# A two-layer hybrid transformer kernel: the residual stream held feature by token instead of token by feature

## The chip, the cores and the metric

The kernel runs on one core of a Trainium2 chip. The metric is device time in microseconds of one execution; lower is better. The kernel before took 808.06 us (median of 3 runs, 807.47 to 808.31). The core has five engines that run their own instruction queues in order: TensorE (PE in the rows; its weight loads are PEld), VectorE (DVE), ScalarE (ACT), GpSimd (POOL) and SyncE (SP), which issues the DMA transfers.

## The reference, cut to what matters

The input is 512 latent tokens `x` and 256 context tokens `ctx`, each of 1024 features, and one conditioning vector for each kind.

```
for layer in range(2):
    shift, scale, gate       = split(silu(c)     @ ada_w[layer] + ada_b[layer], 3)   # 1024 values each
    shift_c, scale_c, gate_c = split(silu(c_ctx) @ ada_w[layer] + ada_b[layer], 3)
    h_l = rmsnorm(x,  norm_g[layer]) * (1 + scale)   + shift
    h_c = rmsnorm(cx, norm_g[layer]) * (1 + scale_c) + shift_c
    # layer 0: latent attention (8 heads) and a bidirectional RG-LRU side by side
    # layer 1: 2-D neighbourhood attention (16 heads), latents only as output
    y_c, y_l = mixer(h_c, h_l)            # (mix * silu(gate path)) @ w_out, 1024 x 1024
    x  = x  + gate   * y_l
    cx = cx + gate_c * y_c                # layer 0 only
return rmsnorm(x, final_norm_g)           # rmsnorm: x * rsqrt(mean(x*x over features) + 1e-6) * g
```

## The kernel before, in words

All 768 tokens (512 latents `LAT`, then 256 context tokens `CTX`) go through the two layers at once. Products that need accuracy are made from operands split into a high part (`...h`, rounded for the fast float32 mode of TensorE) and a rest (`...l`): three matmuls (h x h, h x l, l x h) for each product. `split_raw` (L113) makes the parts of a weight: ScalarE the high part, VectorE or GpSimd the rest, in tiles from small rings (3 raw, 4 high, 4 low) in `t4` (L81). A raw slot is free when the rest has been made, and only then can SyncE issue the next weight's transfer into it.

**Startup.** The residual stream `x` lies token by feature: `x0` to `x5`, 128 tokens x 1024 features each. `norm0` (L327) squares and sums each tile on ScalarE along the features, takes the inverse root for all tokens on VectorE, and scales the tiles. `h_block` (L297) then makes, for each of 8 feature groups `j` and each kind of token, the tiles `hh` and `hl` (128 features x 768 tokens) that the projections read: four or two TensorE transposes into PSUM (`pst`, L302), ScalarE for the high part with scale `am` and shift `as`, VectorE for the difference (L310), GpSimd for the rest (L312). `am` and `as` come from `ada_cols` (L211): matmuls with a 32-column weight, four of them side by side on the columns of the array (`psada`, L205). The projections `z_t` (L134) keep a weight tile still and stream tokens: `psx0` to `psx3` (LRU input), `psg` (gates), `psn` (L578: attention's compressed q, k, v, with the token tile still and 416 weight columns streamed). One projection is 8 x 3 matmuls of 512 and of 256 columns.

**Gates.** `gate_rows` makes the layer's gate as rows (tokens' kind x 256 features), `gate_bc` (L253) spreads them over 128 partitions by a float32 matmul with a selecting weight (`psgt`), since the output projection leaves tokens on the partitions.

**Output projections and seam.** `out_mm` (L1109, `w0oy`, `w1oy`) keeps 128 tokens of the mixed activations `mh`/`ml` still and streams 256 weight columns; `out_add` multiplies by the gate and adds to `x` (two VectorE instructions). Between layer 0 and layer 1 (the "seam") `h_norm`, `x_scale` and `hb1` repeat norm and `h_block` for the new residual, by pairs of token tiles, while TensorE works on the projections left and on the first of layer 1 (`psv`, L1255, and `pskc`, `pskl`). After layer 1 the final norm ends each token tile and stores it, 4 transfers of 128 x 1024.

The order on each engine is that in which the scheduler puts the instructions of the program text; each engine runs its list in order. Tiles come from pools, so a new tile waits for the last reader of the one whose place it takes.

Of the kernel before, what the change touches and what calls it, by code (L numbers as in the profile page):

```python
# [37 lines left out]
NV = 111  # L38
# [5 lines left out]
def build(nc, tc, A, out, dbg=None):  # L44
# [76 lines left out]
    def split_w(name, src, shape, new=None, eng=V):  # L121
        return split_raw(name, load_w(name, src, shape, new), shape, new, eng)
# [25 lines left out]
    pt = pool("pt", 2, space=PSUM)  # L148
# [29 lines left out]
    junk0 = px.tile([128, D], BF16, name="junk0")  # L178
# [5 lines left out]

    sel = cst.tile([128, 2], F32, name="sel")
    iv = ident.rearrange("p (a b) -> p b a", b=32)
    V.tensor_reduce(sel, iv[:, 0:2], AX.X, ALU.add)
    selh = cst.tile([128, 2, 128], F32, name="selh")
    V.tensor_copy(selh, sel.unsqueeze(2).to_broadcast([128, 2, 128]))
    amul = [cst.tile([128, 8, 2], F32, name=f"am{l}") for l in range(2)]  # L190
    ashf = [cst.tile([128, 8, 2], F32, name=f"as{l}") for l in range(2)]
    badd = cst.tile([128, 48], F32, name="badd")
# [18 lines left out]
    def ada_cols(l, ch, raws, pp):  # L211
# [11 lines left out]
        j = 2 * ch  # L223

        def bc(t, i):
            return t[:, i : i + 2].unsqueeze(2).to_broadcast([128, 2, 2])

        V.tensor_tensor(ashf[l][:, j : j + 2], v[:, :, 0:2], bc(vec, V_ADAB + 24 * l + j), ALU.add)
        d = amul[l][:, j : j + 2]
        V.tensor_tensor(d, v[:, :, 2:4], bc(badd, 24 * l + 8 + j), ALU.add)  # L230
        V.tensor_tensor(d, d, bc(vec, V_NG + 8 * l + j), ALU.mult)

    def gate_rows(l, ch, pp, new=None, step=4):

        pm = ada_mm([ada_load(l, 8 + ch, new, step)], pp, f"psgr{l}_{ch}")
        S.activation(grows[:, ch], pm[:, :256], AF.Copy)
        gb = small("rows", f"gb{l}_{ch}", 256)[:2]
        SY.dma_start(gb, A["gateb"][l : l + 1, 256 * ch : 256 * ch + 256].to_broadcast([2, 256]))
        V.tensor_tensor(grows[0:2, ch], grows[0:2, ch], gb, ALU.add)

    def of3(tile):
        def new(n, s, dt, tag):
            if tag == "r" and tile is not th:
# [28 lines left out]
    def rsqrt1(y, a, b, scale):  # L272


        m, t = small("rm", "m1"), small("rt", "t1")
        V.tensor_scalar(m, a, b, scale * 2.0 ** 26, ALU.add, ALU.mult)
        V.tensor_scalar(t.bitcast(I32), m.bitcast(I32), 1, None, ALU.arith_shift_right)
        V.tensor_scalar(
            y.bitcast(I32), t.bitcast(I32), -1.0, float(0x5F3759DF - 2 ** 31), ALU.mult, ALU.add
        )  # L280
        for c in (3.0, 12.0, 768.0):
            V.scalar_tensor_tensor(t, y, m, y, ALU.mult, ALU.mult)
            V.scalar_tensor_tensor(y, t, c, y, ALU.subtract, ALU.mult)
# [1494 lines left out]
```

## Time and profile before

| | |
|---|---|
| median of 3 runs | 808.06 us |
| the profiled execution | 808.98 us |
| its span, first to last instruction | 807.0 us |
| mean granted TensorE clock | 0.986 |
| TensorE busy | 760.4 us, 94% of the span |
| VectorE / ScalarE / GpSimd busy | 505.6 / 419.2 / 167.6 us |

The page's chain that ended last is followed back from the last instruction through what released it; a share of it is a share of the span. Stages in the span: startup and first projections to about 70 us, LRU and the attention's inputs to 200, attention to 340, output projection of layer 0 to 425, the seam to 441, layer 1 to 740, its output projection to 797, the end to 807.

### The profile page before, as it was taken

The page shows a single profiled execution, that of the slowest core. Times are in us where ns is not written, and L with a number is a line of the kernel's source. Part 1 is how long each engine was busy: PE and PEld are TensorE (multiplying, and loading weights), DVE is VectorE, ACT ScalarE, POOL GpSimd, SP SyncE. Part 2 cuts the span into 40 slices and gives each one's busy share as a digit, 9 for nine tenths or more (in the row PEclk, how much of TensorE's full clock was granted, in tenths as well). Part 3 has the DMA queues.
Part 4 walks back from the last instruction along what each step waited for, and adds up shares of the span by engine and source line. Part 5 has one row for each costly group of instructions (what it writes and reads, how often), then busy time and mean ns, then how long its engine had stood idle before and what let it go on. Part 6 is the DMA issues. An engine that isn't in the chain of part 4 may idle for free.

```text
span 807.0 us, 13663 instructions
## 1 busy us (share of the span) xinstructions
PE 760.4 (94%) x5170; PEld 668.9 (83%) x5170; DVE 505.6 (63%) x1083; ACT 419.2 (52%) x820; POOL 167.6 (21%) x208
## 2 busy tenths in 40 slices
PE   3899999997999888999998999999999999999995
PEld 0568998886788678799997889988898889899995
DVE  4547499769478657624466446755654665568755
ACT  4344667763475668632275345544543554457523
POOL 2230000000142548540036002202110111021203
PEclk9999999998999999999999999999999999999998
DMA  8921124410453564145132244224522651335122
GB/s 335 372 88 70 53 91 131 156 41 0 108 141 105 150 183 146 60 135 179 54 141 95 81 129 131 71 73 114 149 92 79 196 170 31 104 115 144 54 79 105
DMA packets 32145, 95.86 MB, mean 119 GB/s; under 512 B 4288, under 2 KB 7504, under 8 KB 32080
## 3 DMA queue, kind: packets, MB, share of 16 engines
q1 hardware_dynamic: 32080, 94.99, 36.7%
q8 instruction: 41, 0.67, 0.3%
q14 instruction: 24, 0.20, 0.1%
HBM read 74.53 MB, written 4.19 MB: 98 GB/s over the span
## 4 chain that ended last, share of the span: by engine, by line
PE 80%; DVE 7%; DMA 5%; ACT 4%; issue 1%; POOL 1%; SPq 1%; DVEq 0%; ACTq 0%; POOLq 0%
PE psg L134 11%; PE w0oy L1109 8%; PE psv L1255 8%; PE psq L134 6%; PE pskl L134 6%; PE w1oy L1109 5%; PE psx L134 4%; PE psn L578 3%; PE pt L1372 3%; PE pskc L134 3%; PE s L745 3%; DMA ada_4r<-ada 2%; PE pg L134 2%; PE s L1331 2%; PE psada L205 2%; PE s L1332 2%
## 5 line engine op out<-in xcount | busy, mean ns | idle before, releaser
L701 POOL TENSOR_SCALAR p<-p,rc 128x512 f32<-128x512 f32 (+1 forms) x96 | 74.7, 780 | 325.9 <-DVE rc L700 313.1
L1339 ACT ACTIVATE p<-s,nm 128x512 f32<-128x512 f32 x64 | 43.9, 687 | 44.5 <-DVE nm L1337 33.3
L1375 DVE TENSOR_TENSOR ptl<-pt,pth 128x512 fp32r<-128x512 f32 x64 | 43.4, 685 | 20.4 <-ACT pth L1374 20.0
L1374 ACT ACTIVATE pth<-pt 128x512 fp32r<-128x512 f32 x64 | 37.2, 596 | 26.9 <-PE pt L1372 23.0
L1337 DVE CUSTOM_DVE_ANT_1 s<-s,bias 128x512 f32<-128x512 f32 x48 | 33.2, 697 | 20.4 <-PE s L1332 20.1
L747 DVE TENSOR_REDUCE nm<-s 128x1 f32<-128x768 f32 x32 | 30.4, 951 | 18.3 <-PE s L745 18.3
L1372 PE MATMUL pt<-ident,p 128*128 128x128 f32 x256 | 39.9, 272 | 0.0
L781 DVE TENSOR_TENSOR pt<-pt,pt 128x512 fp32r<-128x512 f32 x48 | 31.8, 682 | 8.3 <-ACT pt L780 7.8
L749 ACT ACTIVATE p<-s,nm 128x768 f32<-128x768 f32 x32 | 28.9, 903 | 14.1 <-DVE nm L747 14.0
L780 ACT ACTIVATE pt<-pt 128x512 fp32r<-128x512 f32 x48 | 27.2, 597 | 15.4 <-PE pt L818 15.1
L1331 PE MATMUL s<-k,q 128*128 128x256 f32 x128 | 34.0, 288 | 0.4 <-DMA q<-qx 0.4
L1372 PEld LDWEIGHTS pt<-ident,p 128*128 128x128 f32 x256 | 31.1, 140 | 3.6
L1332 PE MATMUL s<-k,q 128*128 128x256 f32 x128 | 33.5, 284 | 0.0
L1355 PE MATMUL po<-pth,v 128*128 128x256 f32 (+1 forms) x96 | 31.9, 338 | 0.0
L680 POOL TENSOR_TENSOR rb<-rb,ropet 128x512 f32<-128x512 f32 x2 | 2.6, 1278 | 138.3 <-DVE rb L678 138.3
L700 DVE RECIPROCAL rc<-rs 128x1 f32<-128x1 f32 x96 | 15.0, 158 | 25.3 <-ACT p L1339 15.5
L1356 PE MATMUL po<-ptl,v 128*128 128x256 f32 (+1 forms) x96 | 29.4, 323 | 0.0
L818 PE MATMUL pt<-ident,p 128*128 128x128 f32 x192 | 28.1, 273 | 0.5 <-DVE pt L781 0.4
L205 PE MATMUL psada<-ada_0r,c 128*32 128x256 f32 x128 | 13.3, 496 | 15.9 <-DMA ada_0r<-ada 9.9
L798 PE MATMUL po<-pt,v 128*128 128x256 f32 x96 | 26.7, 296 | 0.4 <-ACT pt L780 0.2
L799 PE MATMUL po<-pt,v 128*128 128x256 f32 x96 | 26.5, 300 | 0.6 <-DVE pt L781 0.5
L1331 PEld LDWEIGHTS s<-k,q 128*128 128x128 f32 x128 | 24.3, 190 | 2.1 <-DMA q<-qx 0.6
(911 smaller groups left out, 2735.5 us busy)
## 6 DMA issues: line engine op xcount, KB each, us to landing
ada_0r<-ada SPq DMA_DIRECT2D x24, 512.0 KB, 5.5
ada_4r<-ada SPq DMA_DIRECT2D x24, 512.0 KB, 10.1
q<-qx SPq DMA_DIRECT2D x32, 256.0 KB, 4.9
bias<-bias SPq DMA_DIRECT2D x16, 256.0 KB, 3.1
x<-xin SPq DMA_DIRECT2D x6, 512.0 KB, 10.5
xr<-xin SPq DMA_DIRECT2D x12, 256.0 KB, 5.2
x1d<-xr SPq DMA_DIRECT2D x4, 512.0 KB, 2.7
x<-x1d SPq DMA_DIRECT2D x4, 512.0 KB, 3.2
```

The costliest lines, as they stand in the source:

```text
L134: P.matmul(ps, a(k), b[k][:, c], start=(k == 0 and i == 0), stop=(k == nk - 1 and i == 2),)
L701: G.tensor_scalar(p, p, rc, 0.5, ALU.mult, ALU.mult)
L1109: P.matmul(ps[:, j], tok(a[k], t), b, start=(n == i == j == 0), stop=(n == 7 and i == 2), skip_group_check=True,)
L1255: P.matmul(ps, tok(a[k], t), b[:, k % 4], start=(k == 0 and i == 0), stop=(k == 7 and i == 2))
L1331: P.matmul(s[:, :256], lhs, kap, start=(i == 0), stop=False, skip_group_check=True)
L1332: P.matmul(s[:, 256:], lhs, k2[:, CTX], start=False, stop=(i == 1), skip_group_check=True)
L1337: V.tensor_tensor_reduce(sv, sv, bb, -1.0, 3e38, ALU.add, ALU.min, nm)
L1339: S.activation(p, s, AF.Exp, bias=nm, scale=-1.0, accum_out=rsum)
L1355: P.matmul(dst, vv, h, start=first, stop=False, skip_group_check=True)
L1372: P.transpose(ps[:, 128 * j : 128 * j + 128], p1[hd, b][:, 128 * c : 128 * c + 128], ident)
L1374: S.activation(h, ps, AF.Copy)
L1375: V.tensor_tensor(l, ps, f(h), ALU.subtract)
```

## The change

The residual stream is kept feature by token: `x0` to `x7` hold 128 features x 768 tokens, and the host lays out `xin` and takes the output that way (in the transposed shape 1024 x 512). What follows from it:

- **Norms.** ScalarE (two of eight tiles: GpSimd) squares the tiles, TensorE sums over features by matmuls with a 32-column tile of ones (`sq_sum`), `rs_bc` copies the sums, transposes them to tokens on the partitions (`r..t`), adds the four partial sums, takes the inverse root (startup and end: ScalarE's square root, reciprocal and one Newton step; seam: the three-step code of before), and transposes it back spread over 128 partitions (`r..b`) into `rsb`.
- **h_block.** No transposes: VectorE `x * a * rsb` in place, ScalarE adds the shift for `hh`, VectorE makes `hl`. GpSimd has no part in it.
- **Gates** are made as columns (`ada_gate`), like shift and scale; `gate_rows`, `gate_bc` and `psgt` are gone, and `out_add` is one VectorE instruction.
- **Output projections** keep 128 x 128 of the weight still and stream tokens: 512 at a time for layer 0's latents, 256 for its context and for layer 1, which goes in two halves of 256 tokens, each with its own norm and store (16 transfers of 128 x 256 in all).
- **Order.** All `x` loads come first. `psg8` is projected in the startup along with `psx0` and `psx1`. Layer 0's output goes latents first; the latent `hb1` stand among the context's projections, the context's among the first projections of layer 1. Some weight splits move (`w0o2`, `w0o3`, `w1o3`, the rest of `w1k0` to GpSimd).

```
+    def sq_sum(ps, sq, g, n):
+        for j, a in enumerate(sq):
+            P.matmul(ps[32 * j : 32 * j + 32, :n], ones, a, start=(g == 0), stop=(g == 1), skip_group_check=True)
+    def rsqrt1(y, v, scale, n, name):
+        m, t = small("rm", name + "m", n), small("rt", name + "t", n)
+        S.activation(t, v, AF.Sqrt, scale=scale, bias=eps)
+        V.tensor_scalar(m, v, scale, EPS, ALU.mult, ALU.add)
+        V.reciprocal(y, t)
+        V.tensor_tensor(t, y, y, ALU.mult)
+        V.scalar_tensor_tensor(t, t, -0.5, m, ALU.mult, ALU.mult)
+        V.scalar_tensor_tensor(y, t, 1.5, y, ALU.add, ALU.mult)
+    def rs_bc(name, ps, n, part, dst, pp, root=True):
+        nt = n // 128
+        s, r = small("st", f"{name}s", nt), small("st", f"{name}r", nt)
+        S.activation(part[:, :n], ps[:, :n], AF.Copy)
+        t = pp(f"{name}t")
+        for i in range(nt):
+            P.transpose(t[:, 128 * i : 128 * i + 128], part[:, 128 * i : 128 * i + 128], ident)
+        V.tensor_reduce(
+            s, t[:, :n].rearrange("p (t j r) -> p t r j", j=4, r=32)[:, :, 0], AX.X, ALU.add
         )
...
+        b = pp(f"{name}b")
+        for i in range(nt):
+            P.transpose(b[:, 128 * i : 128 * i + 128], r[:, i : i + 1].to_broadcast([128, 128]), ident)
+        S.activation(dst[:, :n], b[:, :n], AF.Copy)
...
+    def h_block(l, j, c, x, rsb, hh, hl, pieces):
         a, s = amul[l][:, j, c : c + 1], ashf[l][:, j, c : c + 1]
...
+        V.scalar_tensor_tensor(x, x, a, rsb, ALU.mult, ALU.mult)
+        for i, o in pieces:
+            S.activation(o(hh), i(x), AF.Identity, bias=s)
+            V.scalar_tensor_tensor(o(hl), i(x), s, f(o(hh)), ALU.add, ALU.subtract)
...
     psx.append(x_t(0))
     psx.append(x_t(1))
+    psg8 = zz3("psg8")
+    z_t(both(psg8), wt.pop(8), hh, hl, 8)
...
+    def out_mm(ps, w, i, mh, ml, ks, c, first=True):
         for n, k in enumerate(ks):
+            wh, wl = (a[:, 128 * i : 128 * i + 128] for a in w[k])
+            for m, (a, b) in enumerate(((wh, mh), (wh, ml), (wl, mh))):
+                P.matmul(
+                    ps, a, b[k][:, c], start=(first and n == m == 0), stop=(n == 7 and m == 2),
+                    skip_group_check=True,
+                )
+    def out_add(ps, x, g):
+        V.scalar_tensor_tensor(x, ps, g, x, ALU.mult, ALU.add)
...
     w0o_prep(1)
     out0(0, 0)
+    w0o_prep(3, of3(tl), 3)
+    out0(2, 0)
+    sum1(0, 0)
+    out0(1, 0)
+    out0(3, 0)
+    sum1(0, 1)
     out0(0, 1)
+    norm1(0)
+    out0(2, 1)
+    sum1(1, 0)
+    hb1(0, 0)
+    hb1(0, 1)
+    hb1(0, 2)
     out0(1, 1)
+    hb1(0, 3)
+    hb1(0, 4)
     out0(3, 1)
...
+    for half in range(2):
+        c = slice(256 * half, 256 * half + 256)
+        pss[half] = oo(f"pss2{half}")
...
+            if j % 4 == 3:
+                sq_sum(pss[half], sq[j - 3 : j + 1], j // 4, 256)
```

Three places show how the order of instructions moves; a name's last number is the tile's own, `x4` a repetition.

**First projections, TensorE.** Before, the list around the first `psx0` matmul reads (`psada0_1`: shift and scale of features 256 to 511; `pst`: transposes of `x`):

```order
L302 MATMUL pst000_225<-ident_67,x0_138 128x128
L302 MATMUL pst000_225<-ident_67,x1_140 128x128
L302 MATMUL pst000_225<-ident_67,x2_142 128x128
L302 MATMUL pst000_225<-ident_67,x3_144 128x128
L205 MATMUL psada0_1_264<-ada0_1_0r_176,c34_100 32x256 x4
L205 MATMUL psada0_1_264<-ada0_1_4r_178,c34_100 32x256 x4
L302 MATMUL pst00512_240<-ident_67,x4_150 128x128
L302 MATMUL pst010_251<-ident_67,x0_138 128x128
L302 MATMUL pst010_251<-ident_67,x1_140 128x128
L302 MATMUL pst010_251<-ident_67,x2_142 128x128
L302 MATMUL pst010_251<-ident_67,x3_144 128x128
L134 MATMUL psx0_466<-hh0_118,w0t0h_236 128x512
```

In the changed kernel (`r0t`, `r0b`: the two sets of transposes of the norm; `psc0_0`: the transposed rows of shift and scale):

```order
L203 MATMUL psada0_0_220<-ada0_0_4r_133,c34_107 32x256 x4
L295 MATMUL r0t_176<-ident_67,part0_140 128x128 x6
L203 MATMUL psada0_0_220<-ada0_4_0r_135,c34_107 32x256 x4
L203 MATMUL psada0_0_220<-ada0_4_4r_137,c34_107 32x256 x4
L305 MATMUL r0b_192<-ident_67,r0r_174 128x128 x6
L216 MATMUL psc0_0_239<-ident_67,rows0_0_237 128x128 x2
L203 MATMUL psada0_1_270<-ada0_1_0r_216,c34_107 32x256 x4
L203 MATMUL psada0_1_270<-ada0_1_4r_218,c34_107 32x256 x4
L138 MATMUL psx0_414<-hh0_200,w0t0h_252 128x512
L203 MATMUL psada0_1_270<-ada0_5_0r_259,c34_107 32x256 x4
L138 MATMUL psx0_414<-hh0_200,w0t0h_252 128x256
L138 MATMUL psx0_414<-hl0_208,w0t0h_252 128x512
```

The transposes of `x` are gone; six and six transposes of the norm stand ahead, and the sums of squares ahead of these.

**The LRU's gates and the second quarter of `psn`, TensorE.** Before, from the last long matmul of `pg011` (an LRU gate) to the first that reads `w0n1h` (second quarter of the attention's input weight) there are 55 rows between:

```order
L134 MATMUL pg011_793<-uh0_656,lgl0_750 128x512
L134 MATMUL psx3_953<-hh2_120,w0t3l_680 128x256
...
L578 MATMUL psn0_1019<-w0n0h_643,hl0_126 128x416
L578 MATMUL psn0_1019<-w0n0h_643,hh1_119 128x416
L578 MATMUL psn0_1019<-w0n0l_645,hh1_119 128x416
L578 MATMUL psn0_1019<-w0n0h_643,hl1_127 128x416
L578 MATMUL psn0_1019<-w0n1h_1025,hh2_120 128x416
```

In the changed kernel 26 rows stand between them:

```order
L138 MATMUL pg011_716<-uh0_637,lgl0_673 128x512
L591 MATMUL psn0_959<-w0n0l_626,hh0_200 128x416
...
L138 MATMUL pg110_820<-uh1_665,lgh1_787 128x512
L138 MATMUL pg110_820<-ul1_666,lgh1_787 128x512
L138 MATMUL pg110_820<-uh1_665,lgl1_789 128x512
L138 MATMUL pg110_825<-uh1_665,lgh1_787 128x256
L138 MATMUL pg110_825<-ul1_666,lgh1_787 128x256
L138 MATMUL pg110_825<-uh1_665,lgl1_789 128x256
L591 MATMUL psn0_959<-w0n1h_965,hh2_202 128x416
```

The projection `psx3` now stands ahead of `pg011`, so less TensorE work lies between the gate and the weight's first use.

**The seam, TensorE.** Before, a token pair's output projection runs with the tokens still:

```order
L1109 MATMUL w0oy01_3928<-w0o00l_3428,mh1_3436 128x256
L1109 MATMUL w0oy01_3928<-w0o00h_3426,ml1_3437 128x256
L1109 MATMUL w0oy01_3928<-w0o00h_3426,mh1_3436 128x256
L1109 MATMUL w0oy01_3928<-w0o00l_3428,mh1_3436 128x256
L1109 MATMUL w0oy01_3928<-w0o00h_3426,ml1_3437 128x256
L1109 MATMUL w0oy01_3928<-w0o00h_3426,mh2_3672 128x256
```

In the changed kernel the sums of squares of layer 0's latents (`pss10`; `sq100`, `sq110` and `sq140` are the squares of feature groups 0, 1 and 4) stand between matmuls of the projections:

```order
L1108 MATMUL w0oy50_3934<-ml3_3763,w0o23h_3658 128x512
L1108 MATMUL w0oy50_3934<-mh3_3762,w0o23l_3660 128x512
L273 MATMUL pss10_3963<-sq100_3855,ones_110 32x512
L273 MATMUL pss10_3963<-sq110_3884,ones_110 32x512
L1108 MATMUL w0oy20_3968<-mh4_2983,w0o14h_3825 128x512
L1108 MATMUL w0oy20_3968<-ml4_2984,w0o14h_3825 128x512
L1108 MATMUL w0oy20_3968<-mh4_2983,w0o14l_3827 128x512
L273 MATMUL pss10_3963<-sq140_3931,ones_110 32x512
L1108 MATMUL w0oy20_3968<-mh5_3118,w0o14h_3825 128x512
L1108 MATMUL w0oy20_3968<-ml5_3119,w0o14h_3825 128x512
L1108 MATMUL w0oy20_3968<-mh5_3118,w0o14l_3827 128x512
```

The eight sum matmuls of the latents stand in five such places, the eight of the context in six, and those of layer 1's first half in eight.

## Rows read from the trace of the kernel before

**Rows 1.** The page: busy time of each engine, and the chain that ended last.

```profile
PE 760.4 (94%) x5170; PEld 668.9 (83%) x5170; DVE 505.6 (63%) x1083; ACT 419.2 (52%) x820; POOL 167.6 (21%) x208
...
PE 80%; DVE 7%; DMA 5%; ACT 4%; issue 1%; POOL 1%; SPq 1%; DVEq 0%; ACTq 0%; POOLq 0%
```

**Rows 2.** Busy time by stretch: engines (instructions), granted clock, DMA share, GB/s.

```profile
0.00:25.40 25.40, 8.49 (x54) 2.48 (x54) 13.99 (x60) 10.71 (x18) 5.92 (x11) 1.00 0.92 351
25.40:70.00 44.60, 43.14 (x298) 31.90 (x299) 25.57 (x51) 17.18 (x27) 10.43 (x15) 1.00 0.52 192
70.00:163.00 93.00, 93.00 (x546) 81.82 (x545) 69.73 (x145) 63.35 (x107) 0.00 (x0) 1.00 0.29 97
163.00:200.00 37.00, 33.02 (x181) 28.11 (x180) 30.43 (x40) 19.59 (x26) 1.29 (x1) 0.91 0.04 15
...
425.00:441.00 16.00, 12.58 (x98) 11.21 (x97) 10.76 (x37) 9.96 (x25) 11.71 (x28) 1.00 0.26 86
...
797.00:807.00 10.00, 0.68 (x6) 0.47 (x4) 5.86 (x32) 3.82 (x6) 0.00 (x0) 0.72 0.52 210
```

**Rows 3.** Chain of waits, 0 to 75 us: start, length, engine and what.

```profile
4.16 8.57 DMA x<-xin
...
12.81 1.16 ACT junk L286 x2
...
56.49 1.00 PE psgr L205 x16
57.49 1.34 PE psn L578 x6
...
61.84 8.04 PE psg L134 x44
```

**Rows 4.** VectorE groups by form, 0 to 60 us: busy us, mean ns, idle before.

```profile
L310 DVE SCALAR_TENSOR_TENSOR htmp<-pst,am,hh 128x512 f32<-128x512 f32 x8 | 6.0, 746 | 4.3 <-ACT hh L305 4.3
L310 DVE SCALAR_TENSOR_TENSOR htmp<-pst,am,hh 128x256 f32<-128x256 f32 x8 | 3.8, 480 | 7.2 <-ACT hh L305 7.2
...
L118 DVE TENSOR_TENSOR w0t0l<-w0t0r,w0t0h 128x1024 fp32r<-128x1024 f32 x1 | 1.2, 1205 | 0.0
...
L231 DVE TENSOR_TENSOR am<-am,vec 128x4 f32<-128x4 f32 x4 | 0.6, 162 | 0.1
```

**Rows 5.** Timeline of TensorE in the startup: a matmul in float32 leaves two records.

```profile
27.32 1.08 PE L205 MATMUL psada<-ada_0r,c 128*32 128x256 f32 x8
...
30.95 0.60 PE L302 MATMUL pst<-ident,x 128*128 128x128 f32 x4
...
31.70 0.64 PE L205 MATMUL psada<-ada_0r,c 128*32 128x256 f32 x8
```

**Rows 6.** Timeline of TensorE beside the gate rows' broadcast at 356 us.

```profile
356.50 1.02 PE L253 MATMUL psgt<-grows,selh 128*128 128x256 f32 x4
```

**Rows 7.** Timelines of TensorE, ScalarE and VectorE, 84 to 93 us.

```profile
84.84 0.39 PE L134 MATMUL pg<-uh,lgl 128*128 128x512 f32 x1
...
86.78 0.62 ACT L490 ACTIVATE lgh<-lgr 128x512 fp32r<-128x512 f32 x1
...
91.88 0.90 ACT L116 ACTIVATE w0n1h<-w0n1r 128x832 fp32r<-128x832 f32 x1 [2.47 <-DMA w0n1r<-w0n]
...
87.43 0.69 DVE L492 TENSOR_TENSOR lgl<-lgr,lgh 128x512 fp32r<-128x512 f32 x1 [4.46 <-ACT lgh L490]
```

**Rows 8.** Chain of waits around the seam, 423 to 450 us.

```profile
427.97 1.43 POOL h1l L312 x4
...
440.87 3.14 PE psv L1255 x24
```

**Rows 9.** End of the program: timeline from 796.9 us, and the tile out.

```profile
797.40 0.28 PE L1109 MATMUL w1oy<-w1o34h,m1l 128*128 128x256 f32 x1
...
802.41 0.48 DVE L1689 SCALAR_TENSOR_TENSOR x<-x,rs,fg 128x256 f32<-128x256 f32 x1
...
DMA to landing us min/median/max: 2.6/2.6/3.1
```

More of the change, by code (lines that the diff above doesn't have):

```diff
@@ L222, in ada_cols, with bc2, ada_hl, ada_gate @@
         )
[L223 to L228, printed above, removed]
-        d = amul[l][:, j : j + 2]
[L230 to L239, printed above, removed]
+        return v
+    def bc2(t, i):
+        return t[:, i : i + 2].unsqueeze(2).to_broadcast([128, 2, 2])
+    def ada_cols(l, ch, raws, pp):
+        v, j = ada_rows(l, ch, raws, pp), 2 * ch
+        V.tensor_tensor(ashf[l][:, j : j + 2], v[:, :, 0:2], bc2(vec, V_ADAB + 24 * l + j), ALU.add)
+        d = amul[l][:, j : j + 2]
+        V.tensor_tensor(d, v[:, :, 2:4], bc2(badd, 24 * l + 8 + j), ALU.add)
+        V.tensor_tensor(d, d, bc2(vec, V_NG + 8 * l + j), ALU.mult)
+    def ada_hl(l, ch, name):
+        return ada_load(l, ch, lambda n, s, dt, tag: t4(n, s, dt, "hl"[n[-2] == "4"]))
+    def ada_gate(l, i, pp):
+        v = ada_rows(l, 8 + 2 * i, [ada_load(l, 8 + 2 * i), ada_hl(l, 9 + 2 * i, "g")], pp)
+        for m in range(2):
+            j = 4 * i + 2 * m
+            V.tensor_tensor(
+                agat[l][:, j : j + 2], v[:, :, 2 * m : 2 * m + 2], bc2(vec, V_ADAB + 24 * l + 16 + j), ALU.add
+            )
     def of3(tile):
         def new(n, s, dt, tag):
-            if tag == "r" and tile is not th:
+            if tag == "r":
                 return t4(n, s, dt, tag)
@@ new lines, in build, with norm0 @@
+    rsb0 = px.tile([128, NT], F32, name="rsb0")
+    def norm0():
+        ps = zz("pssum")
+        part, sq = th("part0"), []
+        for j in range(8):
+            sq.append(th(f"sq{j}"))
+            if j in (2, 5):
+                G.tensor_tensor(sq[j], x_tiles[j], x_tiles[j], ALU.mult)
+            else:
+                S.activation(sq[j], x_tiles[j], AF.Square)
+        pieces = [(ps[:, :512], NL), (ps[:, 512:], NC)]
+        for g in range(2):
+            for (o, n), c in zip(pieces, (LAT, CTX)):
+                sq_sum(o, [a[:, c] for a in sq[4 * g : 4 * g + 4]], g, n)
+        rs_bc("r0", ps, NT, part, rsb0, zz3)
@@ L402, in build, with gate_t @@
         dump(f"hl{j}", f(hl[j]))
-    close("ptmp", "pada", "px", "pt", "pa")
+    close("pada", "px")
+    pmix = pool("pmix", 8)
+    tmix = tile3(pmix, "mix")
+    mix = [tmix(f"mix{p}") for p in range(4)] + [None] * 4
+    def gate_t(ft, p, ps=None):
+        if ps is None:
+            ps = zz(f"psg{ft}")
+            z_t(both(ps), wt.pop(ft), hh, hl, 8)
+        if mix[p] is None:
+            mix[p] = tmix(f"mix{p}")
+        S.activation(mix[p], ps[:, :NT], AF.Tanh, scale=0.5)
+        V.scalar_tensor_tensor(mix[p], mix[p], 1.0, ps[:, :NT], ALU.add, ALU.mult)
+    gate_t(8, 4, psg8)
+    close("pzz3", "pa")
     ptt = pool("ptt", 3, space=PSUM)
```

451 lines of the change are left out of this document (157 added, 294 removed).

## The prediction

> **What bounds the kernel now.** I read the page first: TensorE is busy for 760.4 of 807.0 us and carries 80% of the chain that ended last [rows 1]. So an edit counts if it takes matmuls out of TensorE's list or shortens a wait in it; the other engines count only where TensorE waits for them. Next the busy times by stretch [rows 2]: TensorE is full from 70 to 163 us, and its idle time lies in four places: the startup (8.5 of the first 25.4 us busy, 43.1 of the next 44.6), the end of the LRU (33.0 of 37.0 from 163 us), the seam (12.6 of 16.0 from 425 us) and the last 10 us (0.7 busy). The change touches the first and the last two of these. Then the chain, to see what the startup waits for: the arrival of `x` until 12.7 us, squares, root, scaling, and only at 61.84 us the projection `psg8`, which ends 8.04 us later at 69.88 [rows 3]. In the seam the chain goes through GpSimd's `h1l` and ends in a wait for the first `psv` at 440.87 [rows 8]. After the last matmul at 797.40 there are 9.6 us of norm and stores [rows 9].
>
> **Startup.** The end of the third projection (`psx0`, `psx1`, `psg8`) is the mark. Before it is 69.88, and TensorE has by then done 1.0 us of `psgr` and 1.3 us of `psn` that come later in the changed kernel [rows 3]: 67.6 like for like.
> After: the eight `x` tiles are as many bytes (3.1 MB) as what landed by 12.7 us before (two weight halves, four tiles), so `x7` lands at about 12.7. Its square takes 0.8 us (1.06 for 1024 columns within the 1.16 of [rows 3], scaled to 768). Four float32 matmuls of 32 x 256 side by side take 0.45 us at 31.70, and about 0.85 at 27.32 [rows 5]; TensorE has so far hardly run, so I take the slower figure: the last sums of 512 and 256 columns cost 1.7 + 0.85. The copy of 768 columns is 0.85 (estimate from the same square), six transposes at twice 0.11 [rows 5] are 1.3, six small VectorE and ScalarE steps at 0.16 [rows 4] with their hand-overs 1.2, the second six transposes with the `psada` ahead of them 1.8, the copy to `rsb` 0.85: `rsb` at 22.3. First `x*a*rsb` and first high part (0.75 each): first `psx` at 24.
> From there VectorE needs 8 x (2 x 0.75 + 2 x 0.48) = 19.7 us for `h_block`, 3 x 1.2 and 1.7 for weight splits and 2.0 for `am`, `as` [rows 4]: it ends near 49.6. TensorE needs three projections of 8.5 (44 of the 48 matmuls took 8.04, so a pair of 512 and 256 columns takes 0.35 to 0.37; split by columns, 0.23 and 0.12), ten groups of `psada` at 0.45 and 0.6 of transposes: 30.6. That is the longer list, so TensorE decides once it is fed: 24 + 30.6 = 54.6. Bounds: it runs at half speed for some 6 us, as at 27.32 (a loss of 3, between 0 and 6); I take 57.6. The new operations, two-input instructions from SBUF with a column, have no row; by the PSUM form they cost 0.75 and 0.48, the bounds are 0.5 and 1.0 of a microsecond for 512, and at the upper one VectorE ends at 54, still inside. Gain 10.0. The fourth projection then needs a slot that the first frees, a copy and a split: 0.8 back. **Net -9.2**, between -5 and -13.
>
> **TensorE's list after that.** Out: 48 transposes in the seam at 0.11 = 5.2; 12 `psgt`, of which two take 0.8 to 1.0 at 356.50 [rows 6], = 4.8; 192 pairs of 256-column matmuls become one of 512 (0.24 against 0.23): 1.7. In: the sums. The order shows them not four at a time but in five places for the latents, six for the context, eight for layer 1's first half. A float32 matmul of 256 columns alone takes 0.4 [rows 6], as long as four side by side [rows 5]; so a place costs 0.86 at 512 columns and 0.43 at 256: 4.3 + 2.6 + 3.4, and 0.4 for the second half's first group. With 24 more transposes (2.6) that is 13.3 in and 11.7 out: **+1.6**. If matmuls parted by others still overlapped, it would be -5.3.
>
> **A new wait at the LRU gates.** `w0n1r` is issued into the raw slot that `lgl1` frees. Before: gate matmul at 84.84, `lgh` at 86.78, `lgl` 87.43 to 88.12, transfer, `w0n1h` 91.88 to 92.78 [rows 7]: 7.7 us from where TensorE could go on to the finished weight. Before, 55 matmuls (9.9 us by the prices above) cover it. After, 26 stand between: five `psn` at 0.2 [rows 3], twelve short and nine long ones, 4.5 us. TensorE waits 7.7 - 4.5 = **+3.2** (bounds 0, if ScalarE and VectorE are ahead, and 4). All behind it on TensorE waits too.
>
> **Seam.** Gone are GpSimd's part and the chain token pair by token pair; 3.4 us of idle time are there to win in 425 to 441 [rows 2], some 5 with latencies. After: part copy, root (twelve steps of 0.16 to 0.2) and transposes end about 15 us after the last latent matmul, because `r10b` stands among the context's projections; these and the context's own sums last 21 us and hide it. Then VectorE makes latents at 1.7 us per feature group against TensorE's 1.44 for four `psv`: TensorE starts at 21, the last group is ready at 30 to 33, TensorE reaches it at 31. So 0 to 2 us of waiting there and about 1 for the context. **-2.5**, between 0 and -4.
>
> **End.** After the last matmul: add 0.5, square 0.45, sum 0.45, copy 0.4, transposes 0.3, six small steps 1.1, transposes 0.3, copy 0.4, hand-overs 0.7, six scalings of 0.48, issue and landing (2.6 us for 512 KB, 2.3 estimated for the last 128 KB) [rows 9]: 10 to 12.5, against 9.6. All tokens of the half wait for one chain. **+2.0**.
>
> **Sum.** -9.2 + 1.6 + 3.2 - 2.5 + 2.0 = -4.9: span 802.1. With the 2.0 us around it the profiled execution's 808.98 becomes 804.1; this execution is 0.9 above the median of 808.06, so I predict 803.
>
> **Rivals.**
> *Slower: the clock stays low in the startup.* TensorE is fed in pieces from 24 to 29 us, then is ahead of VectorE in places. If it stays at half speed until VectorE's list ends at 49.6, instead of until 30, it loses half of 19.6: +9.8, 812 to 813. It becomes slower than before from 10 us of such delay. For it: 0.91 granted in 163 to 200, after the LRU's wait [rows 2]. Against it: at 27.32 half speed, at 31.70 full, with transposes and waits between [rows 5] (the granted clock reads 1.00 in both, so the durations decide). The Trainium skill ("TensorE: Matmul & The Clock Gate", HAM oscillation) says that matmul bursts with waits for data between them fall back to the low clock each time; by that rule this rival is the forecast. The 0.91 agrees, the 93 of 93 us at 1.00 show only that dense work keeps the clock. Chance 0.13.
> *No gain: the ten microseconds are not passed on.* Between 163 and 200 us VectorE is busy 30.4 of 37 us [rows 2], with the LRU's chain. If that chain, not TensorE, sets when attention starts, a part of 5 us is lost: 808. Against it: 69.7 of 93 before it, so VectorE has room and starts earlier too. Chance 0.15.
> *More gain.* The wait at the gates is covered (-3.2) and the sums overlap or are hidden in waits (-3 to -7): 794 to 797. For it: TensorE's seam still has waits to fill. Chance 0.2.
> *No effect* is excluded: the transposes and the GpSimd step are gone from the text.
>
> **How the numbers follow.** The likeliest case, as summed, 0.52, with its own range of 798 to 807. What a measurement of this kernel can tell from no change is about 0.2%, 1.6 us: faster is below 806.4, slower above 809.7. Faster: 0.2 of the better case and 0.45 of the likeliest, 0.65. Same: 0.07 and half of the no-gain case, 0.14. Slower: the clock and the other half of the no-gain case, 0.21. Range 793 to 813.
>
> **What would show it.** Right, if `psg8` ends at 56 to 60 us; TensorE waits 2 to 4 us for `w0n1h`; sums alone take 0.8 us each; 425 to 441's counterpart loses 1 to 3 us; the end lasts 11 to 12.5. Wrong, if VectorE's `h_block` steps cost over 1 us, the half speed lasts past 35 us, or attention starts as late as before.

## The result and the profile after

The changed kernel takes 826.51 us (median of 4 runs, 825.97 to 832.3), the kernel before 807.76 beside it: a ratio of 1.0248, 95% interval 1.0202 to 1.0294. I had said 803, range 793 to 813: wrong in sign, and outside the range. The profiled execution has a span of 824.6 us. Single runs of either kernel differ by some microseconds on several of the chips (of before, 803 to 814), so below a part is read from marks inside the traces first and from medians second.

The page's busy line and chain by engine, after, against [rows 1]:

```profile
PE 772.9 (94%) x4994; PEld 655.2 (79%) x4994; DVE 503.6 (61%) x1049; ACT 410.6 (50%) x792; POOL 135.2 (16%) x158
...
PE 80%; DVE 9%; DMA 5%; ACT 4%; issue 2%; SPq 0%; POOL 0%; DVEq 0%; ACTq 0%
```

TensorE has 176 instructions fewer and is busy 12.5 us longer. The count alone says little, as 192 pairs of matmuls became one each. Four marks that any trace has, worked out from TensorE's timelines (end of `psg8`; last `w0oy`; last `w1oy`; end of the span), tell in which stage. The last column is where the terms of my sum that fall in a stage had put it:

| stage | before | after | forecast |
|---|---|---|---|
| start to the end of `psg8` | 69.8 | 58.2 | 57.6 |
| to the last `w0oy` | 350.6 | 358.8 | about 360 |
| to the last `w1oy` | 377.1 | 395.2 | about 373 |
| to the end | 9.5 | 12.4 | 11.5 |

(Second forecast: 350.6 + 2.3 of `psgr` and `psn` moved there + 0.8 + 3.2 + 6.9 of sums + 1.3 of transposes - 3.2 of `psgt` - 1.7 of merged pairs. Third: 377.1 - 5.2 - 1.6 + 3.8 + 1.3 - 2.5.) Up to the seam the totals came out near the forecast. (For the second stage that is a weak test: in the traces of runs 1, 3, 6, 7 and 9, whose instructions are the same up to there, it takes 356 to 364 us.) 22 of the 24 us by which I was wrong lie between the seam and the last matmul, in layer 1, which I had thought of as "TensorE's list": so many matmuls out, so many in.

**Startup and LRU.** Busy time by stretch of the changed kernel, against [rows 2]:

```profile
0.00:25.40 25.40, 15.56 (x99) 5.52 (x103) 8.55 (x41) 12.50 (x18) 4.00 (x11) 0.93 0.91 346
...
20.00:23.50 3.50, 3.30 (x24) 1.63 (x22) 1.85 (x7) 1.29 (x2) 0.00 (x0) 0.52 1.05 414
...
25.40:58.20 32.80, 32.68 (x229) 23.92 (x221) 21.68 (x47) 12.72 (x23) 0.00 (x0) 1.00 0.52 200
...
417.00:433.00 16.00, 16.00 (x115) 13.99 (x114) 10.83 (x34) 4.34 (x12) 0.56 (x2) 1.00 0.20 67
```

and the three waits of TensorE, 0.92, 0.58 and 1.35 us, at the gates and at `w0n1h`, against [rows 7]:

```profile
84.62 0.50 PE L138 MATMUL pg<-uh,lgh 128*128 128x512 f32 x1 [0.92 <-ACT lgh L512]
...
87.21 0.39 PE L138 MATMUL pg<-uh,lgh 128*128 128x256 f32 x1 [0.58 <-ACT tg L523]
...
90.25 0.65 PE L591 MATMUL psn<-w0n1h,hh 128*128 128x416 f32 x2 [1.35 <-ACT w0n1h L118]
```

The granted clock is low from 20.0 to 23.5 us only, ahead of the first `psx` matmul at 24.74, and 1.00 from there to the end of `psg8`, so the rival of a slow startup is out. The first `w0oy` starts at 334.3 us instead of 340.7, so the startup's gain was handed on past the LRU and attention, and the rival of no gain is out too. In the seam, 12.6 of 16.0 us busy before, TensorE is now never idle.

**The last mix.** Layer 1's output projection multiplies eight mixes, and the eighth (`m1h7`, `m1l7`) is ready last, after the last `po`. Timelines of TensorE, ScalarE, VectorE and GpSimd there; in brackets stands the idle time before, and who ended it:

```profile
764.76 0.28 PE L1313 MATMUL po<-ptl,v 128*128 128x256 f32 x1
768.24 0.58 PE L1108 MATMUL w1oy<-m1h,w1o04h 128*128 128x256 f32 x1 [3.20 <-ACT m1h L1348]
768.62 0.41 PE L1108 MATMUL w1oy<-m1h,w1o14h 128*128 128x256 f32 x1
768.84 0.41 PE L1108 MATMUL w1oy<-m1h,w1o26h 128*128 128x256 f32 x1
...
770.35 0.58 PE L1108 MATMUL w1oy<-m1l,w1o04h 128*128 128x256 f32 x1 [0.68 <-DVE m1l L1349]
...
774.53 0.28 PE L1108 MATMUL w1oy<-m1h,w1o00h 128*128 128x256 f32 x1
774.64 0.28 PE L1108 MATMUL w1oy<-m1l,w1o00h 128*128 128x256 f32 x1
...
765.08 0.59 ACT L706 ACTIVATE cb<-po 64x512 f32<-64x512 f32 x1 [1.43 <-PE po L1313]
767.56 0.63 ACT L1348 ACTIVATE m1h<-mix 128x512 fp32r<-128x512 f32 x1 [1.90 <-DVE mix L708]
...
765.70 0.69 DVE L707 TENSOR_TENSOR cb<-po,cb 64x512 f32<-64x512 f32 x1 [1.33 <-ACT cb L706]
766.43 1.10 DVE L708 TENSOR_TENSOR mix<-mix,cb 64x512 f32<-64x512 f32 x1
768.23 2.07 DVE L1349 TENSOR_TENSOR m1l<-mix,m1h 128x512 fp32r<-128x512 f32 x1 [0.70 <-ACT m1h L1348]
...
764.63 2.35 POOL L122 TENSOR_TENSOR w1o30l<-w1o30r,w1o30h 128x1024 fp32r<-128x1024 f32 x1
766.93 2.82 POOL L122 TENSOR_TENSOR w1o34l<-w1o34r,w1o34h 128x1024 fp32r<-128x1024 f32 x1
```

From the last `po` a chain of copy, add, product and copy takes 3.5 us, and TensorE has nothing to do in it. When it goes on, a matmul starts every 0.21 us until 774.4, then every 0.12. The granted clock by stretch:

```profile
764.90:770.00 5.10, 1.57 (x7) 1.14 (x5) 3.57 (x3) 1.22 (x2) 4.85 (x2) 0.77 0.66 205
770.00:775.00 5.00, 4.65 (x23) 4.65 (x24) 2.49 (x6) 0.42 (x1) 0.00 (x0) 0.55 0.00 0
775.00:780.00 5.00, 5.00 (x40) 4.46 (x39) 0.97 (x2) 0.81 (x3) 0.00 (x0) 1.00 0.00 0
```

It is 0.55 in the five microseconds after the wait, near the lower of the two levels (1.2 of 2.4 GHz). So the wait is paid twice: 3.20 + 0.68 of idleness, and 24 matmuls that take 5.6 us instead of 2.9 (24 x 0.12), 2.7 more: 6.6 us. In the kernel before no wait of TensorE stands in the view of waits from 741 us to the end. The orders of the two programs show why: 210 matmuls of this projection don't need the last mix and stand ahead of the first that does, 33 of them behind the last `po` (33 x 0.12 = 4.0 us, longer than the chain). In the changed kernel it is 105, all used up before the last `po`:

```
4240 L1313 MATMUL po115_8127<-ptl1153_8165,v133_7405 128x256
4241 L1108 MATMUL w1oy00_8218<-m1h7_8180,w1o04h_7906 128x256
4242 L1108 MATMUL w1oy20_8273<-m1h7_8180,w1o14h_7922 128x256
```

The banks are the same five in both kernels. But before, a bank's two token tiles alternated at each `k`, so 7 of 8 `k` of both halves of a bank could run early; now the two feature groups of a bank are computed one after the other, and the second can't begin before the first has had the last mix.

**Other waits in layer 1.** The view of waits of TensorE, 480 to 734 us, after (before it has one row, of 0.4 us):

```profile
PE psada L203 <- DMA ada_0r<-ada: 2.4, 1, 2.4
PE psc L216 <- ACT rows L213: 1.1, 1, 1.1
PE psada L203 <- DMA ada_4r<-ada: 0.6, 1, 0.6
```

These are the gate rows, made for two chunks at once where before there was one. Behind the longest of them, which ends at 625.7 us, the granted clock is 0.50 from 627.7 to 631.0.

**Sums.** A sum among other matmuls, at 256 and at 512 columns, on TensorE's timeline:

```profile
368.73 0.39 PE L1108 MATMUL w0oy<-mh,w0o23l 128*128 128x512 f32 x1
369.05 1.05 PE L273 MATMUL pss<-sq,ones 128*32 128x512 f32 x4
370.03 0.50 PE L1108 MATMUL w0oy<-mh,w0o14h 128*128 128x512 f32 x1
...
779.08 0.28 PE L1108 MATMUL w1oy<-m1h,w1o14l 128*128 128x256 f32 x1
779.29 0.62 PE L273 MATMUL pss<-sq,ones 128*32 128x256 f32 x2
779.84 0.38 PE L1108 MATMUL w1oy<-m1h,w1o20h 128*128 128x256 f32 x1
780.06 0.28 PE L1108 MATMUL w1oy<-m1l,w1o20h 128*128 128x256 f32 x1
```

From the `w1oy` before it to the second one behind is 0.98 us instead of two pitches of 0.12, so one sum of 256 columns takes 0.74; at 512 columns a place takes about 1.2. I had 0.43 and 0.86. All eight lone sums of layer 1's first half cost the same 0.74, whichever of the four column groups they write. The kernel before has a lone float32 matmul of 256 columns too, the gate rows' `psgt`, 128 columns wide in the array:

```profile
368.94 0.28 PE L1109 MATMUL w0oy<-w0o04l,mh 128*128 128x256 f32 x1
369.06 0.59 PE L253 MATMUL psgt<-grows,selh 128*128 128x256 f32 x2
...
369.61 0.28 PE L1109 MATMUL w0oy<-w0o04h,mh 128*128 128x256 f32 x1
```

By the same count it takes 0.67 - 0.24 = 0.43, my price. So the sums cost 0.31 more than a float32 matmul that is 128 columns wide.

**End.** VectorE's last steps, against [rows 9]; the last `w1oy` ends at 812.3:

```profile
812.37 0.48 DVE L1114 SCALAR_TENSOR_TENSOR x<-w1oy,ag,x 128x256 f32<-128x256 f32 x1 [0.95 <-PE w1oy L1108]
817.27 3.40 DVE L1646 SCALAR_TENSOR_TENSOR x<-x,vec,rsb 128x256 f32<-128x256 f32 x6 [1.00 <-ACT rsb L306]
```

From the last add to the first scaling it is 4.9 us, forecast 4.6; six scalings take 3.40, 0.57 each and not 0.48: the two beside GpSimd's scalings take 0.95 and 0.94, the other four 0.47 or 0.48.

### The profile page after: what moved, and what is told of

It is laid out like the page before. It is cut to its first block, busy times and chain, and to the rows that moved or that the text cites. A ratio compares the mean times of both kernels' runs of the same rounds, so it can differ in the third digit from the quotient of the medians.

```text
span 824.6 us, 13175 instructions
## 1 busy us (share of the span) xinstructions
PE 772.9 (94%) x4994; PEld 655.2 (79%) x4994; DVE 503.6 (61%) x1049; ACT 410.6 (50%) x792; POOL 135.2 (16%) x158
## 4 chain that ended last, share of the span: by engine, by line
PE 80%; DVE 9%; DMA 5%; ACT 4%; issue 2%; SPq 0%; POOL 0%; DVEq 0%; ACTq 0%
PE psg L138 12%; PE w0oy L1108 8%; PE psv L1212 8%; PE psq L138 6%; PE pskl L138 5%; PE w1oy L1108 5%; PE psx L138 4%; PE pt L1329 3%; PE pskc L138 3%; PE s L757 3%; PE psn L591 3%; PE psada L203 3%; DMA ada_4r<-ada 2%; PE s L1288 2%; PE pss L273 2%; PE s L1289 2%
## 5 line engine op out<-in xcount | busy, mean ns | idle before, releaser
L713 POOL TENSOR_SCALAR p<-p,rc 128x512 f32<-128x512 f32 (+1 forms) x96 | 77.7, 813 | 342.8 <-DVE rc L712 314.3
L712 DVE RECIPROCAL rc<-rs 128x1 f32<-128x1 f32 x96 | 14.9, 158 | 25.5 <-ACT p L1296 15.9
L1114 DVE SCALAR_TENSOR_TENSOR xr<-w0oy,ag,xr 128x512 f32<-128x512 f32 (+1 forms) x16 | 9.6, 615 | 29.4 <-PE w0oy L1108 28.1
```

What stands on the lines that cost most here:

```text
L713: G.tensor_scalar(p, p, rc, 0.5, ALU.mult, ALU.mult)
```

## The experiments

Two theories after the result. A: the loss is the uncovered last mix. B: the loss is spread over what the change put on the engines (sums, gate rows, GpSimd's weight copies). All times are medians; the kernel before took 807.8 to 808.7 in the four groups of runs. Behind each run's time stand the range of its single runs, and its ratio to the kernel before with the 95% interval. Stage lengths are those of the table above, and "tail" is its last stage; each is read from one trace.

**1. Alternate the feature groups.** One bank's two feature groups at each `k` instead of one after the other:

```diff
-            out_mm(ps, w1o[j // 2], i, mh, ml, [0, 3, 5, 2, 4, 1, 6, 7], c, i == 0)
...
+        for n, k in enumerate(ks):
+            for i in range(2):
+                wh, wl = (a[:, 128 * i : 128 * i + 128] for a in w[k])
+                for m, (a, b) in enumerate(((wh, mh), (wh, ml), (wl, mh))):
...
```

> The two feature groups that share a PSUM bank in layer 1's output projection are computed side by side over k instead of one after the other; same matmuls, same result. Theory A (TensorE runs out of matmuls that do not need the last mixed tile: 105 stand ahead of the first that reads m1h7 in the changed kernel, 210 in the kernel before, and here 210 again): the wait of 3.2 us at 768 us, the 0.7 us after it and the 3.1 us lost at half clock go, and fillers take the small waits from 740 us on: 816 to 819 us against 826.5. Theory B (the chain to m1h7 and m1l7 itself is late because GpSimd's weight split holds VectorE): the wait stays, 825 to 827.

824.29 us (819.58 to 827.92), 1.0195 [1.0144, 1.0245]. From the last `w0oy` to the last `w1oy` it takes 389.2 instead of 395.2, but the tail takes 18.2 instead of 12.4. The tail shows why, VectorE then ScalarE:

```profile
813.56 3.25 DVE L1657 SCALAR_TENSOR_TENSOR x<-x,vec,rsb 128x256 f32<-128x256 f32 x8
...
810.24 1.28 ACT L281 ACT_TABLE_LOAD   x1
```

The first half's last bank now ends with the second half's, so its norm, the table load for its root, and its eight scalings stand ahead of the second half's root. What was won went into a new wait (`r21b` 4.4 us). The median is 5 us above what A had said and just below B's range, so it doesn't decide. The trace does in part: the wait for `m1h`, which B had expected to stay, fell from 3.2 to 1.8 us, and that for `m1l` is gone.

**2. Cheap sums.** The sums stand where they stood, but in the fast float32 mode with one 32-column group (the squares are rounded to that mode):

```diff
-            P.matmul(ps[32 * j : 32 * j + 32, :n], ones, a, start=(g == 0), stop=(g == 1), skip_group_check=True)
+            P.matmul(ps[:32, :n], ones, a, start=(g == j == 0), stop=(g == 1 and j == 3), skip_group_check=True)
```

(The startup's sums are changed in the same way.)

> The sums of squares are taken in the fast float32 mode (squares rounded to it, one 32-column group for all eight tiles), so a lone sum costs 0.25 to 0.3 us instead of 0.75 (256 columns) and 1.1 (512). Theory A (each lone sum is TensorE time: 5 places at 512, 14 at 256 columns): 8 to 10 us less, 816 to 819. Rival (the sums mostly fill waits for other engines): less than 3 us, 824 to 827.

825.54 us (824.59 to 826.48), 1.0217 [1.0197, 1.0238]. The median is where the rival had put it. The sums are what they were meant to be, one pitch:

```profile
778.16 0.28 PE L1106 MATMUL w1oy<-m1h,w1o14l 128*128 128x256 f32 x1
778.27 0.28 PE L273 MATMUL pss<-sq,ones 128*32 128x256 f32 x1
778.39 0.28 PE L1106 MATMUL w1oy<-m1h,w1o20h 128*128 128x256 f32 x1
```

The first to the last `w0oy` takes 77.1 us instead of 82.7. In layer 1 nothing is left of it: TensorE comes earlier to a bank that VectorE has not emptied yet, a wait that the changed kernel does not have:

```profile
PE w1oy L1106 <- DVE x L1112: 2.9, 1, 2.9
```

In the startup, with its sums one after another in one group, the first `psx` starts at 28.4 us, against 24.1 to 25.5 in the runs with the startup of the changed kernel, and `psg8` ends at 61.4.

**3. No weight copies on GpSimd.**

```diff
-    w1o_prep(3, pew, eng=G, heng=G)
+    w1o_prep(3, pew)
```

> The last weight block of layer 1's output projection is split by ScalarE and VectorE again, not by GpSimd. Theory B (GpSimd's two-input instruction makes VectorE's m1l take 2.07 us instead of 0.69, and mix 1.10 instead of 0.67): 2 to 4 us less, 822 to 825. Theory A: at most 1.5 us less (the 0.7 us wait and a little of the 3.2), 825 to 826.5, since the same fillers are missing.

830.47 us (828.11 to 837.15), 1.0288 [1.0238, 1.0338]: not faster, and above what either theory had said; its trace is of its longest run. The wait for `m1h` is the same 3.2 us, that for `m1l` 0.5 instead of 0.7. `m1l` itself takes 0.68 us now instead of 2.07, but VectorE makes the copies ahead of it. So GpSimd's copies slow VectorE's `m1l`, but this is not what costs the time.

**4. Gate weights of the LRU in slots of their own.** The raw tiles of the LRU gates get two slots outside of the ring that `w0n1r` waits for.

```diff
-        raw = t4(f"lgr{ft}", (4, 128))
+        raw = plm.tile([128, 4, 128], F32, tag="lgr", name=f"lgr{ft}", bufs=2)
```

> The raw gate weights of the LRU get two slots of their own, so w0n1r no longer waits for lgl1. If the waits at 84 to 91 us (0.92 + 0.58 + 1.35) come from that slot, 1.4 to 2.9 us go and are passed on: 823.5 to 825. Rival (the LRU's VectorE chain sets the start of attention, so nothing is passed on): 826 to 827.

827.62 us (825.71 to 831.07), 1.0244 [1.0213, 1.0276]. Nothing was gained, as the rival had it. The three waits are gone, and two others came, in the view of waits from 75 to 110 us:

```profile
PE psn L591 <- ACT w0n3h L118: 2.7, 1, 2.7
PE pg L138 <- ACT tg L523: 1.2, 1, 1.2
```

That is 3.9 us in place of 2.85: the wait for a weight of `psn` moved from `w0n1h` to `w0n3h`, two loads on. So the slot is not all that makes the weights late; what else does was not tested.

**5. The changed kernel's order in the kernel before.** The cleanest test of A: only the order of one loop, and nothing else of the change.

```diff
-        for n, k in enumerate(ks):
-            for j, t in enumerate(ts):
+        for j, t in enumerate(ts):
+            for n, k in enumerate(ks):
```

(shortened, and for layer 1's projection alone)

> The kernel before, with one edit: in layer 1's output projection the two token tiles that share a PSUM bank are computed one after the other over all eight k, as the changed kernel does with its two feature groups, instead of alternating at each k. Nothing else of the change is in it. Theory A (the loss of the changed kernel sits where TensorE waits for the last mix, because only 105 instead of 210 matmuls of this projection can run ahead of it): the same hole opens here, some 3 us of waiting and then half clock, 8 to 12 us in all, 816 to 820 against 808. Rival B (the loss is of the changed kernel's sums, gates or GpSimd's weight copies): no change, 807 to 810.

817.62 us (816.87 to 819.82), 1.0113 [1.0078, 1.0147]. The last `w0oy` to the last `w1oy` takes 385.3 instead of 377.1. The wait for the last mix is there, 2.8 us long up to 772.0, behind 105 matmuls of this projection, with a low clock behind it. The other wait, for `m1l`, is new as well, but stands at 748.5, at the sixteenth matmul. The views of waits and of busy time:

```profile
PE w1oy L1113 <- ACT m1h L1395: 2.8, 1, 2.8
PE w1oy L1113 <- DVE m1l L1396: 1.2, 1, 1.2
```
```profile
772.00:777.00 5.00, 5.00 (x29) 5.00 (x30) 0.67 (x1) 0.00 (x0) 0.00 (x0) 0.66 0.53 210
```

A is shown: the order of this loop alone costs 8 to 9 us in the kernel before (8.2 by the stage, 8.9 by the medians). It is not the whole 18.8.

**6. Alternation, and GpSimd out of the last weights,** which puts the first half's last bank ahead of the second half's (edits 1 and 3 together).

> The changed kernel with the two feature groups of a bank alternating at each k, as in the first experiment, and the last weight quarter split on ScalarE and VectorE instead of GpSimd, which lets the order of the program finish the first token half before the second (in the first experiment GpSimd's late weights put the first half's norm into the tail). Theory A: the 9.3 us won between the first and the last matmul of this projection stay, and the tail is that of the changed kernel (12.4), so 814 to 818. Rival B (what is won there comes back as another wait): 822 to 826.

822.61 us (822.12 to 825.51), 1.0178 [1.0148, 1.0208], as rival B had it. It takes 389.0 from the last `w0oy` to the last `w1oy`, near the 389.2 of run 1; the tail is 15.7. Most of what the tail lost is VectorE again, with the first half's scalings ahead of the second half's last two additions:

```profile
804.03 3.26 DVE L1657 SCALAR_TENSOR_TENSOR x<-x,vec,rsb 128x256 f32<-128x256 f32 x8 [2.00 <-ACT rsb L306]
807.20 0.87 DVE L1125 SCALAR_TENSOR_TENSOR x<-w1oy,ag,x 128x256 f32<-128x256 f32 x2
```

**7. Gate rows chunk by chunk,** at the four places of before:

```diff
-    ada_gate(1, 1, zt)
+    ada_gate1(1, 2, zt)
...
+    ada_gate1(1, 3, zt)
```

> The changed kernel with the gate rows of layer 1 made one 256-column chunk at a time at the four places of the kernel before, instead of two chunks at two places. If the waits for the gate weights (2.40 and 0.56 us at 625.68 and 626.88) and for the rows (1.11 at 570.07) are due to the grouping, layer 1 loses 3 to 4 us less, some of it with two transposes more: 822.5 to 824.5 against 826.5. Rival: the loads wait for the same slots wherever they stand, 826 to 828.

826.46 us (823.29 to 831.05), 1.0223 [1.0178, 1.0268]: by the median nothing, where I had expected 2 to 4. In the trace the waits for the loads are gone and the one for the rows is 0.5, and the last `w0oy` to the last `w1oy` takes 392.7, 2.5 less. The spread of these four runs is three times that.

**8. All of these together** (1, 2, 3, 7).

> All that seemed to help in one kernel: groups of a bank alternating at each k, last weight quarter on ScalarE and VectorE, sums of squares in the fast float32 mode in one 32-column group (the squares rounded to it), gate rows of layer 1 chunk by chunk. If the parts add up: 826.5 - 9.3 - 3 - 3 = 809 to 813, level with the kernel before or a little above. If they are given back: 818 to 824.

811.12 us (808.84 to 816.09, 10 runs), 1.0047 [1.0018, 1.0075], inside what I had expected. The last `w0oy` to the last `w1oy` takes 379.8, against 389.0 without sums and gates (run 6). By TensorE's records, 5.3 of these 9.2 us are the gate rows with their waits and 4.2 the sums, which gave nothing alone. In the stage before, the sums give 5.6 us (from the first to the last `w0oy`, against run 6). The tail is 15.4, the startup 62.8: both longer than the 12.4 and 58.2 of the changed kernel.

**9. The last stage alone, mended further:** 1 and 3, the low-weight product ahead of the one with `m1l` at each `k`, and five of the first half's scalings on GpSimd.

```diff
-                for m, (a, b) in enumerate(((wh, mh), (wh, ml), (wl, mh))):
+                for m, (a, b) in enumerate(((wh, mh), (wl, mh), (wh, ml))):
...
+    GF = ((1, 2, 4, 5, 6), (2, 5))
```

> The changed kernel with only its last stage mended: groups of a bank alternating at each k, at each k the product with the low weight ahead of the one with the low mix (so that two products per bank run before the late m1l, as in the kernel before), the last weight quarter on ScalarE and VectorE, and five of the first half's eight final scalings on GpSimd, so that VectorE is free for the last additions. Theory A: of the 16.5 us lost in this stage 4 to 6 are left and the tail is 12: 812 to 816. Rival B: as in the run with alternation alone, most comes back in the tail: 820 to 824.

820.97 us (819.64 to 824.74), 1.0166 [1.0113, 1.022]. Expectation A was missed by 5; B's range was met. The wait for `m1l` fell to 0.4, but the stage took 388.1, since the sums and the gate rows still cost what they did; and moving scalings to GpSimd slowed the ones that VectorE kept, GpSimd and VectorE side by side:

```profile
802.22 4.06 POOL L1638 TENSOR_TENSOR x<-x,rsb 128x256 f32<-128x256 f32 x5 [3.94 <-ACT rsb L306]
802.51 1.82 DVE L1640 SCALAR_TENSOR_TENSOR x<-x,vec,rsb 128x256 f32<-128x256 f32 x2
```

0.91 each, against 0.41 in run 6 (eight in 3.26). The tail is 15.1.

**10. Everything,** with the startup's sums as in the changed kernel.

> The same last stage, with the sums of the later norms in the fast float32 mode and the gate rows of layer 1 chunk by chunk; the startup's sums as in the changed kernel. Against the combined kernel at 811.1 that gives back some 4 us of startup (27.2 lost there against 21 to 23.5 with the sums as changed), 1 to 2 us of waiting for m1l and 2 of the tail: 803 to 807, below both kernels. If these are given back: 810 to 812.

807.18 us (801.37 to 813.13, 11 runs) against 808.09: 0.9978 [0.994, 1.0016]. That is 19 us less than the changed kernel and just above what I had expected, 803 to 807, below both kernels: it is level with the kernel before, and that it is faster isn't shown. Its trace is of one of its longest runs, 812.04. Waits of its last stages:

```profile
PE pss L280 <- ACT sq L1672: 2.4, 1, 2.4
PE w1oy L1134 <- ACT m1h L1374: 1.6, 1, 1.6
```

## Why the prediction was wrong

**Startup: the total right, two of its parts by luck.** The mark was forecast at 57.6, inside 56 to 60, and came at 58.3 (the last `psg8` matmuls start at 57.74 and take 0.52); before it was 67.6 like for like [rows 3]. The first `psx` came at 24.74, forecast 24. But 3 us of the forecast were half speed behind that point, and none fell there: the granted clock is 1.00 from 23.5 us on. In their place TensorE's list from the first `psx` to the end of `psg8` took 33.5 us and not 30.6: the three projections 27.3 instead of 25.5, `psada` 5.4 instead of 4.5, `psc` 0.7. The two errors cancel. In runs 1 and 7, with the same startup, the clock is low from 24.1 to 30.9 us, and `psg8` ends at 60.4. The rivals of a slow clock and of no gain are out.

**The slot: right in size, not in place.** +3.2 forecast, all of it at `w0n1h`; 1.35 was there, and 0.92 + 0.58 at two gate matmuls ahead of it that have no term in my sum, 2.85 in all. A slot of its own (run 4) took these waits away and brought 3.9 us of others. So the agreement is in part luck.

**The sums: undersized.** 0.43 and 0.86 a place became 0.74 and about 1.2, 0.3 more at either length. The price of a float32 matmul among others was right for one that is 128 columns wide (0.43 for `psgt` in the kernel before); I had taken it for a lone one of 32 columns as well, and had counted no time for changing over. The Trainium skill ("TensorEngine Tiling (Array Packing)", Key Properties) says that a change of tiling mode drains TensorE; that speaks for the gap, and I had not weighed it. The trace agrees in part: a 32-column sum in the fast mode and in one group costs no more than its pitch of 0.12 (run 2), so 32 columns alone do not bring the cost; the float32 passes alone do not either (`psgt`), nor does the column group (all four cost the same). The 0.3 comes where float32 and 32 columns meet; why is not shown. In the projection of layer 0 the total still came out near the forecast (358.8 for about 360 in that stage). That is in part luck too: ten of the seam's 48 transposes, 1.1 us, lay in that stage, and I had taken all of them out of the next.

**Seam: right, and a little better.** TensorE is busy for 16.0 of 16.0 us there. In the transposes and the waits of `psv`, 9.0 us are gone, forecast 5.2 + 2.5.

**End: right.** +2.0 forecast, +2.9 measured (12.4 against 9.5).

**What failed is a step that isn't in the sum.** "TensorE's list after that" counted the matmuls of layer 1's projection as moved at the same price, and did not ask which of them may run before the last mix. I had looked for new waits where the diff adds a load, and not where it turns a loop inside out. The diff shows the turned loop (a feature group over all eight `k`, and two groups to a bank), and the order shows 105 against 210. The price could have been read from the trace before: 33 matmuls of 0.12 cover a chain of 3.5 us, and nothing covers it without them. No rival of mine had this mechanism either. In the same step the gate rows' loads had no wait, and the sums were too cheap.

**What layer 1's 22 us are made of.** Each matmul of TensorE is given the time from the end of the one before it to its own end, idle time included, and this is added up by tile from the last `w0oy` to the last `w1oy`. The change from before to after, against the terms of my sum, in us:

| part | forecast | measured |
|---|---|---|
| layer 1's projection: `w1oy`, and the `po` among it (5.8 of it waits) | 0 | +12.2 |
| gate rows (4.1 of it waits) | 0 | +4.2 |
| sums | +3.8 | +6.6 |
| transposes of norms and gate rows | +1.3 | +1.7 |
| `psgt` | -1.6 | -1.7 |
| the seam: `pst`, and the waits of `psv` | -7.7 | -9.0 |
| all other matmuls (1.3 of it waits for the weights of `psg`) | 0 | +4.0 |
| together | -4.2 | +18.0 |

So the projection makes more than half of the 22 us, the gate rows 4, the sums 3. The turned loop is shown for 7 to 8 of the projection's 12.2: in these rows run 5 adds 7.4 to the kernel before, and alternation takes 7.3 (run 1) and 7.6 (run 6) away from the changed kernel. Some 5 are left even with alternation. In run 8 there are two waits (1.4 for `m1h` and 1.0 for `m1l`), in run 10 two (1.6 and 0.4), with a low clock behind them; run 10:

```profile
770.00:775.00 5.00, 3.70 (x21) 3.50 (x22) 3.84 (x6) 1.43 (x4) 0.00 (x0) 0.80 0.46 154
775.00:780.00 5.00, 5.00 (x39) 4.97 (x39) 3.08 (x8) 1.84 (x5) 1.82 (x4) 0.86 0.00 0
```

The traces show why: 210 matmuls stand ahead of the last mix again, but in runs 1, 6, 8, 9 and 10 195 to 197 of them are spent before the last `po`, against 177 in the kernel before, so 13 to 15 are left for the chain of 3.5 us instead of 33. Why they are spent sooner is open, and so is most of the 4.0 of the other matmuls. All this rests on single traces. What each part costs depends on the others: sums alone and gate rows alone gave nothing in the medians; in run 2 TensorE waited for the next late thing. With all of them mended the kernel is level with the one before (run 10), although `psg8` ends 9 us earlier (60.4): in its trace layer 0 takes 5.8 us more up to the last `w0oy`, layer 1 takes 2.1 more, and the tail 4.8 more (14.3).

The Trainium skill ("TensorE: Matmul & The Clock Gate", HAM oscillation) had been the sentence beside my slower rival: matmul bursts with waits between them fall to the low clock. I had applied it to the startup, where in the trace above the clock was low for 3.5 us ahead of the projections and not in them. The trace agrees at the last mix, after one wait of 3.2 us: 0.55 granted, 0.21 us a matmul instead of 0.12.

## What to carry to other kernels

When a change turns a loop, count for each late operand how many instructions may run before it, in the order of both programs, and set that against the chain that makes the operand: the count of matmuls can stay the same while the cover halves. A wait of TensorE in a full stretch can cost more than its length, as the clock may fall behind it (3.9 us of waiting cost 6.6 here). A part that gives little when mended alone is not cleared: edits that gave some 2 us at most one by one gave 15 together.

## What the runs showed of the hardware that I had not expected

VectorE's instructions with two inputs from SBUF slow down beside GpSimd's: `m1l` took 2.07 us beside a GpSimd subtraction of 2.82, where [rows 7] have 0.69 for a subtraction of that shape and run 3, without GpSimd, 0.68 for `m1l` itself; a scaling of 256 columns took 0.91 instead of 0.41 (run 9). The Trainium skill ("SBUF — State Buffer", SBUF: two separate sides) says that the two share a port pair that one of them holds for a whole instruction. The times agree: `mix` and `m1l` each end 0.55 us after the GpSimd subtraction that they overlap (766.98 and 769.75), and `cb<-po,cb`, with one of its two inputs in PSUM, took its 0.69 beside the same subtraction. Moving work to an idle GpSimd was therefore no gift to a busy VectorE.

A float32 matmul with a 32-column weight, alone among others, took 0.3 us more of TensorE than one with 128 columns (0.74 and 0.43 at 256 columns streamed), while in the fast float32 mode one with 32 columns took no more than its pitch (0.12, run 2).
